# Two modulation maps of layer 1 summed by chains on VectorE instead of matmuls, with new ranks for the first feed-forward

## The chip, the cores and the metric

The kernel runs on one core of a Trainium2 chip. The metric is device time in microseconds (us) of one execution; the kernel before takes 2758.88 us in the median of 3 runs (2758.69 to 2758.89). Work is issued to five in-order engines: TensorE (PE, with its weight loads as PEld), VectorE (DVE), ScalarE (ACT), GpSimd (POOL) and SyncE (SP), which here issues all the transfers.

## The reference

The program is a trunk of two transformer layers over 1024 latent tokens and 256 context tokens, width 1024, in float32. Every layer first computes its modulation: six vectors of 1024 (shift, scale and gate for the attention and for the feed-forward) from one conditioning vector, once for the latent tokens and once for the context tokens.

```python
mod = silu_c @ w_mod[i] + b_mod[i]
mod_c = silu_cc @ w_mod[i] + b_mod[i]
sh1, sc1, gt1, sh2, sc2, gt2 = jnp.split(mod[:, None, :], 6, axis=-1)
sh1c, sc1c, gt1c, sh2c, sc2c, gt2c = jnp.split(mod_c, 6, axis=-1)
h = modulate(rmsnorm(x, g_attn[i]), sh1, sc1)
hc = modulate(rmsnorm(ctx, g_attn[i]), sh1c, sc1c)
```

So a map `v` (0 to 5) is a product of a row of 1024 with a matrix of 1024 x 1024. Layer 1 is the last layer. Its context tokens only deliver keys and values, so only the maps 0 and 1 (shift and scale of the attention) are needed for both rows, latent and context; the maps 2 to 5 are needed for the latent row alone.

After the attention, a layer has a gated feed-forward: an up-projection to 2 x 2816, a convolution over three positions, `a * silu(g)`, and a down-projection, for the latent tokens and in layer 0 for the context tokens too.

## The kernel before

Layer 0 and layer 1 each run in stages: attention, then the feed-forward. In the feed-forward of layer 0 (called ffn0) there follow each other the output projection of the attention, the context tokens' feed-forward (PE tiles `uc<-h2c` and `dnc`), the latent up-projection in 22 positions, and the down-projection in five sweeps.

Float32 weights are multiplied in three products: each weight block is loaded raw (`wraw`), rounded by ACT to its high part (`whi`) and its rest taken by DVE (`wlo`), and PE multiplies high by high, high by low and low by high. The up-projection also uses sums and differences of blocks (a fast scheme with seven block products in place of eight): per position DVE forms four sums `s`, takes the low parts of four weight blocks (`wlo`, three of 1024 columns and one of 512), and adds three products that come out of PSUM to the results `c`. PE runs 84 matmuls of 512 columns per position, named `ua`, `ud` and `uc`. Then `plan_u` (line 2017) makes the convolution: ACT starts a tile `u` from `c`, DVE adds the two other taps for both halves (four instructions on 1023 columns), ACT takes the SiLU, DVE multiplies, and DVE forms the blocks `ghit` and `glot` that go out to memory.

The tiles `c` and `u` come from one ring of eight slots (`x_tile`, line 1453, tag "x": the up results' ring). Raw loads come from a ring of three (`rpool`, line 280).

The maps of layer 1 are computed inside ffn0, under the up-projection. There are two ways to do it.

- By matmuls, `plan_mod` (line 405) with `mod_mm` (line 341): the activated conditioning vectors, padded to 32 columns (`cpad`), are the weights, and a 128-row slice of the matrix streams past them in four pieces of 256 columns. Two slices are loaded (`wm`), then eight matmuls of 32 x 256 run together; they sum up in a PSUM bank (`mod`). Eight slices make a map for both rows at once. The kernel before does maps 0 and 1 of layer 1 in this way (line 2084).
- By chains, `plan_mod_chain` (line 457): ACT multiplies the first slice by the conditioning value of each partition (`macc<-wm`), DVE adds the seven other slices times theirs with one SCALAR_TENSOR_TENSOR of 1024 columns each, and at the end four matmuls with a block of ones sum over the partitions (`mod<-macc,ones`). The kernel before does maps 2 to 4 in this way, for one row, with the running sum `macc` in one slot of the ring of eight.

In both ways ACT copies the bank, two transposes (`mod<-idr,modsb`) turn the sums, and DVE adds the bias (`modc`).

The order of all this is set when the program is built. A planner (`Sched`, line 97) takes every operation with an estimated duration and a key, lets each engine take the ready operation with the smallest key, and respects the slots of each ring; the engines then run in the order that comes out. `RANKS` (line 61) is a table of offsets to single operations' keys, one table for each stage, addressed by the number of the operation in the stage (applied at line 2261 for ffn0). All instructions go through one recording helper, so all of them carry its line, L51.

Of the kernel before, what the change touches and what calls it, by code (L numbers as in the profile page):

```python
# [11 lines left out]
F32 = mybir.dt.float32  # L12
# [5 lines left out]
P = 128  # L18
D = 1024
KT = 8  # L20
# [18 lines left out]
class InOrder:  # L39
# [7 lines left out]
    def __getattr__(self, name):  # L47
        f = getattr(self.eng, name)

        def call(*a, **k):  # L50
# [25 lines left out]
    ffn0={321: 16.4, 346: 3.3, 364: -15.4, 382: 3.9, 387: 4, 388: -8.1, 389: -5.4, 433: -24.5, 499: 13.3, 502: 17,  # L76
          503: -8.5, 519: 1.9, 548: 28.3, 571: 47.3, 1150: -18.3, 3223: -3.9, 3317: 2.1, 3398: 3.9, 3445: -3.9,
          3455: 9.6, 3469: 6.9, 3609: 20, 3613: 6.8},
    sw={6: -33, 8: -15, 11: 29.2, 14: 18.5, 67: -2.8, 73: -2.8, 74: 57.2, 141: -74.9, 152: 3.4, 162: 17.4, 168:
# [189 lines left out]
def trunk_kernel(ctx, tc, xperm, xtok, xseq, cc, wmod0, wmod, bmod, gnorm, na_wqkv, na_gq, na_gk, na_bias, na_wo,  # L269
# [3 lines left out]
    act, dve, pool, pe, dma = [InOrder(tc, e) for e in (nc.scalar, nc.vector, nc.gpsimd, nc.tensor, nc.sync)]  # L273

    cpool = ctx.enter_context(tc.tile_pool(name="const", bufs=1))
# [23 lines left out]
    dve.memset(cpad, 0.0)  # L299
    dma.dma_start(cpad[:, :, 0:2], cc)  # L300
    ones = cpool.tile([P, P], F32, name="ones")
    make_identity(nc, ones)
    idr = cpool.tile([P, P], F32R, name="idr")
    dve.tensor_copy(idr, ones)
# [842 lines left out]
    sc = Sched(dict(CAPS, klt=1))  # L1147
# [286 lines left out]
    def ffn(l, opj, xt1, todo):  # L1434
# [8 lines left out]
        sc = Sched(dict(b=8, raw=3, w=WBUFS, x=8, sr=SRB, g=GB, g2=GB, sq=2), {"b", "raw", "w", "x", "sr", "g", "g2", "sq"})  # L1443
# [6 lines left out]
        def bank(nm):  # L1450
            return ps.tile([P, 512], F32, tag="b", name=nm, bufs=8)

        def x_tile(nm):
            return fp.tile([P, 1024], F32, tag="x", name=nm, bufs=8)
# [18 lines left out]
        KU = KC + (8.8 * (FT + 1) if not last else 0.0)  # L1473
# [606 lines left out]
                plan_diffs()  # L2080
            plan_up(pos)
        if not last:
            for n in range(0, 16, 2):
                plan_mod(sc, 1, n // KT, n % KT, lambda: bank("mod"), "b", KU + 10 * n - 8, 3.0, True)
            for v in range(2, 5):
                plan_mod_chain(sc, v, 1, lambda: bank("mod"), "b", KU + 80 * v - 8, 10.0, 2.0, lambda: x_tile("macc"))
        else:
            plan_mod_chain(sc, 5, 1, lambda: bank("mod"), "b", KU + 150, 10.0, 2.0, lambda: x_tile("macc"))

# [297 lines left out]
    slabs = Slabs(sw_wqkv, WL1)  # L2387
    NSLAB = 2
    ffn(0, op0, None, [0, 1])
    gqk, sink, bandt, rc, rs = [C1[n] for n in ("gqk", "sink", "bandt", "rc", "rs")]  # L2390
    xs[1] = Parts([lo_part("x1", F32) for _ in range(4)], 2)
# [10 lines left out]
    sc = Sched(dict(CAPS, qraw=3, xl=4), {"raw"})  # L2402
# [403 lines left out]

    c1.close()
    ffn(1, op1, Parts(xt1, 4), [1])


# [93 lines left out]
def build(arrays):  # L2904
    import concourse.bacc as _bacc

    nc = _bacc.Bacc("TRN2", target_bir_lowering=False, num_devices=1, dynamic_dma_scratch_size=64)
    args = [nc.dram_tensor(f"in_{n}_dram", arrays[n].shape, mybir.dt.from_np(arrays[n].dtype), kind="ExternalInput").ap()
            for n in _INS]
    args.append(nc.dram_tensor("out_0_dram", (P, KT, T), F32, kind="ExternalOutput").ap())  # L2910
    with tile.TileContext(nc) as tc:
        trunk_kernel(tc, *args)
    return nc
# [10 lines left out]
```

## Time and profile before

| | before |
|---|---|
| median of 3 runs | 2758.88 us (2758.69 to 2758.89) |
| the profiled execution | 2759.63 us, its span 2757.8 us |
| granted TensorE clock | 0.999 |
| output projection of layer 0 | about 708 to 798 us of the span |
| context feed-forward of layer 0 | about 798 to 998 us |
| up-projection of layer 0 | about 985 to 1423 us |
| down-projection of layer 0 | about 1423 to 1634 us |

In the rows of the views, an instruction stands with its start, its duration, its engine, `out<-in`, the shape, and in brackets the idle time of its engine before it and what ended that. A duration is longer than the distance to the next instruction, because the next one starts before the last has drained; where a price is wanted, the distance between starts is the one to take. A busy share of PE counts those overlaps, so a busy PE need not be at its peak; the distance between starts tells that too.

### The profile page before, as it was taken

What the parts mean: (1) busy time and instruction counts of PE and PEld (TensorE: products, weight loads), DVE (VectorE), ACT (ScalarE), POOL (GpSimd) and SP (SyncE); (2) the same over time, 40 slices, a digit from 0 to 9 for tenths busy, and PEclk for the clock granted to TensorE, in tenths of its full rate; (3) what the DMA queues carried; (4) which work ended last, traced back from release to release, by engine and by line L of the source; (5) the groups of instructions that cost most, each with busy time, mean ns of one, the idle gap of its engine ahead of it and who ended that gap; (6) DMA issues with size and microseconds to landing.
All of it is one profiled execution on the core that took longest, in us unless ns stands there. A gap on an engine that the chain in (4) does not pass through costs nothing.

```text
span 2757.8 us, 45386 instructions
## 1 busy us (share of the span) xinstructions
PE 2731.3 (99%) x16073; PEld 2431.8 (88%) x16073; DVE 2291.1 (83%) x5005; ACT 1701.8 (62%) x3333; POOL 418.3 (15%) x684
## 2 busy tenths in 40 slices
PE   8999999999999999999999999999999999999999
PEld 7999999999889987788888888999988888888887
DVE  6888878888779678798998698888997989888766
ACT  6877777778556554455554457888874655555443
POOL 1222122223100000000000017546430000000000
PEclk9999999999999999999999999999999999999999
DMA  7222222224745544444476561010254234334745
GB/s 286 80 85 82 73 72 84 91 76 124 263 139 191 184 159 154 153 155 141 159 236 238 172 217 45 14 35 19 77 193 144 73 115 145 123 108 148 256 149 191
DMA packets 144868, 375.60 MB, mean 136 GB/s; under 512 B 22144, under 2 KB 35072, under 8 KB 143232
## 3 DMA queue, kind: packets, MB, share of 16 engines
q1 hardware_dynamic: 144640, 372.70, 40.8%
q8 instruction: 126, 2.06, 0.3%
q14 instruction: 102, 0.84, 0.1%
HBM read 305.59 MB, written 67.04 MB: 135 GB/s over the span
## 4 chain that ended last, share of the span: by engine, by line
PE 70%; DVE 3%; ACT 1%; issue 1%; DMA 0%; POOL 0%; SPq 0%; DVEq 0%; POOLq 0%; ACTq 0%
PE ua L51 17%; PE dn L51 15%; PE uc L51 12%; PE mm L51 6%; PE oacc L51 5%; PE ud L51 4%; PE pt L51 3%; PE pv L51 2%; PE s L51 2%; PE dnc L51 2%; PE u L51 1%; DVE S L51 1%; DVE ptlo L51 0%; PE mod L51 0%; DVE wlo L51 0%
## 5 line engine op out<-in xcount | busy, mean ns | idle before, releaser
L51 ACT ACTIVATE whi<-wraw 128x512 fp32r<-128x512 f32 (+1 forms) x264 | 212.9, 808 | 181.4 <-PE uc L51 55.2
L51 DVE TENSOR_TENSOR wlo<-wraw,whi 128x512 fp32r<-128x512 f32 (+1 forms) x264 | 240.5, 913 | 39.9 <-ACT whi L51 39.4
L51 DVE TENSOR_TENSOR ptlo<-pt,pthi 128x512 fp32r<-128x512 f32 (+2 forms) x384 | 223.0, 596 | 36.1 <-ACT pthi L51 33.8
L51 ACT ACTIVATE S<-S,m 128x640 f32<-128x640 f32 (+3 forms) x288 | 221.2, 770 | 35.8 <-DVE m L51 29.0
L51 PE MATMUL dn<-ghi,whi 128*128 128x512 f32 x616 | 239.9, 390 | 0.0
L51 PE MATMUL dn<-ghi,wlo 128*128 128x512 f32 x616 | 239.7, 389 | 0.0
L51 PE MATMUL dn<-glo,whi 128*128 128x512 f32 x616 | 239.6, 389 | 0.0
L51 ACT ACTIVATE pthi<-pt 128x512 fp32r<-128x512 f32 (+2 forms) x384 | 195.1, 524 | 55.1 <-PE pt L51 35.5
L51 DVE SCALAR_TENSOR_TENSOR u<-c,cv,u 128x1023 f32<-128x1023 f32 x176 | 222.2, 1279 | 3.4 <-ACT u L51 2.9
L51 ACT ACTIVATE whi<-s 128x1024 fp32r<-128x1024 f32 (+1 forms) x116 | 109.0, 940 | 164.0 <-PE uc L51 110.8
L51 ACT ACTIVATE ghi<-graw 128x512 fp32r<-128x512 f32 x154 | 96.4, 630 | 176.4 <-PE dn L51 103.5
L51 PE MATMUL pt<-idr,S 128*128 128x128 f32 x1280 | 195.2, 274 | 2.2 <-DVE qt L51 1.1
L51 PE MATMUL mm<-whi,h0hi 128*128 128x384 f32 x480 | 171.9, 358 | 0.4 <-ACT qraw L51 0.4
L51 DVE TENSOR_TENSOR glo<-graw,ghi 128x512 fp32r<-128x512 f32 x154 | 105.6, 689 | 72.0 <-ACT ghi L51 66.3
L51 PE MATMUL mm<-wlo,h0hi 128*128 128x384 f32 x480 | 162.0, 337 | 0.0
L51 PEld LDWEIGHTS pt<-idr,S 128*128 128x128 f32 x1280 | 149.6, 140 | 10.5 <-DVE ptlo L51 1.9
L51 POOL TENSOR_TENSOR qy<-qv,mhalf 128x4 f32<-128x4 f32 (+1 forms) x112 | 123.2, 1101 | 160.9 <-DVE qv L51 157.5
L51 POOL TENSOR_TENSOR n1y<-n1v,mhalf 128x4 f32<-128x4 f32 (+1 forms) x8 | 8.3, 1041 | 895.3 <-DVE n1v L51 895.3
L51 DVE TENSOR_TENSOR wlo<-s,whi 128x1024 fp32r<-128x1024 f32 (+1 forms) x116 | 124.4, 1075 | 21.3 <-ACT whi L51 21.1
L51 PEld LDWEIGHTS dn<-glo,whi 128*128 128x128 f32 x616 | 115.6, 188 | 24.1
L51 PEld LDWEIGHTS dn<-ghi,whi 128*128 128x128 f32 x616 | 115.6, 188 | 23.9
L51 PEld LDWEIGHTS dn<-ghi,wlo 128*128 128x128 f32 x616 | 115.6, 188 | 23.9
(392 smaller groups left out, 8856.0 us busy)
## 6 DMA issues: line engine op xcount, KB each, us to landing
wraw<-in_w_up_dram SPq DMA_DIRECT2D x132, 512.0 KB, 3.9
wm<-in_wmod_dram SPq DMA_DIRECT2D x80, 512.0 KB, 4.0
wraw<-in_w_down_dram SPq DMA_DIRECT2D x44, 512.0 KB, 3.8
graw<-g_dram SPq DMA_DIRECT2D x44, 512.0 KB, 4.5
wraw<-in_w_down_dram SPq DMA_DIRECT2D x88, 256.0 KB, 3.2
graw<-g_dram SPq DMA_DIRECT2D x66, 256.0 KB, 2.8
slab<-in_na_wqkv_dram SPq DMA_DIRECT2D x32, 384.0 KB, 3.8
woraw<-in_na_wo_dram SPq DMA_DIRECT2D x24, 512.0 KB, 4.5
```

Source lines behind the costliest of these rows:

```text
L51: r = f(*a, **k)
```

## The change

The two rows of maps 0 and 1 are now made by chains. Each of the two maps has two running sums, one for each row, and so two slots of the ring of eight; each of the slices 1 to 7 is added by two DVE instructions, and slice 0 is scaled by two ACT instructions. At the end eight matmuls sum over the partitions; so that the two rows land in the first and the second of the 32 columns, their weights are 32 columns out of a new tile `pick` of 33, which holds a column of ones among zeros. Maps 2 to 4 stay as they are. The table of ranks for ffn0 has 53 entries instead of 23, none of them kept with its value; the numbers that it refers to move too, because the chains have other operations than the matmuls had.

```diff
-    ffn0={321: 16.4, 346: 3.3, 364: -15.4, 382: 3.9, 387: 4, 388: -8.1, 389: -5.4, 433: -24.5, 499: 13.3, 502: 17,
...
+    ffn0={363: -13, 370: -3.9, 387: 24.1, 608: -73.6, 1117: 14.4, 1405: 25.9, 1438: -7.5, 1450: 26.8, 1480: -7.5,
...
     ones = cpool.tile([P, P], F32, name="ones")
+    pick = cpool.tile([P, 33], F32, name="pick")
+    dve.memset(pick, 0.0)
+    dve.memset(pick[:, 1:2], 1.0)
...
         if not last:
-            for n in range(0, 16, 2):
-                plan_mod(sc, 1, n // KT, n % KT, lambda: bank("mod"), "b", KU + 10 * n - 8, 3.0, True)
-            for v in range(2, 5):
-                plan_mod_chain(sc, v, 1, lambda: bank("mod"), "b", KU + 80 * v - 8, 10.0, 2.0, lambda: x_tile("macc"))
+            for v in range(5):
+                plan_mod_chain(sc, v, 2 if v < 2 else 1, lambda: bank("mod"), "b", KU + 80 * v - 8, 10.0, 2.0, lambda: x_tile("macc"))
```

The body of `plan_mod_chain` was there before, and is not changed. Its part for two rows, which ran in no program until now:

```python
for r in range(rows):
    def first(e, r=r, j=j):
        acc[r] = acc_tile()
        act.activation(acc[r], st[j], AF.Copy, scale=cpad[:, j, r:r + 1])

    def link(e, r=r, j=j):
        dve.scalar_tensor_tensor(out=acc[r], in0=st[j], scalar=cpad[:, j, r:r + 1], in1=acc[r], op0=ALU.mult, op1=ALU.add)
...
for r in range(rows):
    for g in range(4):
        pe.matmul(mod_acc[1, v][32 * g:32 * g + 32, :256], ones[:, :32] if rows == 1 else pick[:, 1 - r:33 - r],
                  acc[r][:, g * 256:(g + 1) * 256], start=r == 0, stop=r == rows - 1, skip_group_check=True)
```

What moves on the engines is shown at three places. On PE, in the early up-projection, a group of eight matmuls of the maps stands between products of two positions, once per position for eight positions; here is the first of the kernel before.

```order
L51 MATMUL ua_14387<-b22hi_14159,whi_14359 128x512
L51 MATMUL ua_14387<-b22lo_14173,whi_14359 128x512
L51 MATMUL ua_14387<-b22hi_14159,wlo_14360 128x512
L51 MATMUL mod_14372<-wm_14416,cpad_83 32x256 x4
L51 MATMUL mod_14372<-wm_14479,cpad_83 32x256 x4
L51 MATMUL ua_14540<-b1hi_11614,whi_14435 128x512
L51 MATMUL ua_14540<-b1lo_11625,whi_14435 128x512
```

All eight groups are gone, and after each of the two chains stands one group, here the first, with the two running sums as streams and the pick tile as weights.

```order
L51 MATMUL ua_14810<-t12lo_12256,whi_14838 128x512
L51 MATMUL ua_14810<-t12hi_12005,wlo_14839 128x512
L51 MATMUL mod_14963<-macc_14240,pick_87 32x256 x4
L51 MATMUL mod_14963<-macc_14252,pick_87 32x256 x4
L51 MATMUL ua_14810<-t12hi_12005,whi_14838 128x512
L51 MATMUL ua_14810<-t12lo_12578,whi_14838 128x512
```

The group stands in the fifth position, and the second one in the ninth; between positions 5 and 12 the products of neighbouring positions are also interleaved where they stood one position after the other before.

On DVE, a stretch around the convolution of the third position of the kernel before: low parts of weights (`wlo`), additions of products (`c`), taps of the convolution (`u`).

```order
L51 TENSOR_TENSOR wlo_14639<-s_14620,whi_14638 128x1024
L51 TENSOR_TENSOR c1_14609<-c1_14609,ua_14540 128x512
L51 TENSOR_TENSOR c1_14609<-c1_14609,uc_14604 128x512
L51 TENSOR_TENSOR wlo_14664<-s_14615,whi_14663 128x1024
L51 SCALAR_TENSOR_TENSOR u_14670<-c1_14609,cv_102,u_14670 128x1023
L51 TENSOR_TENSOR wlo_14685<-wraw_14556,whi_14684 128x512
L51 SCALAR_TENSOR_TENSOR u_14670<-c1_14609,cv_102,u_14670 128x1023
L51 SCALAR_TENSOR_TENSOR u_14692<-c0_14566,cv_102,u_14692 128x1023 x2
L51 TENSOR_TENSOR u_14692<-u_14692,u_14670 128x1024
L51 TENSOR_TENSOR c0_14719<-c0_14719,ud_14715 128x512
```

The same place of the changed kernel, with four links of the two chains (`macc`) in it.

```order
L51 SCALAR_TENSOR_TENSOR u_14689<-c0_14555,cv_105,u_14689 128x1023
L51 TENSOR_TENSOR wlo_14703<-wraw_14600,whi_14702 128x512
L51 TENSOR_TENSOR c0_14696<-c0_14696,ud_14692 128x512
L51 SCALAR_TENSOR_TENSOR u_14689<-c0_14555,cv_105,u_14689 128x1023
L51 SCALAR_TENSOR_TENSOR macc_14240<-wm_14667,cpad_83,macc_14240 128x1024
L51 TENSOR_TENSOR u_14689<-u_14689,u_14654 128x1024
L51 SCALAR_TENSOR_TENSOR macc_14252<-wm_14667,cpad_83,macc_14252 128x1024
L51 SCALAR_TENSOR_TENSOR macc_14240<-wm_14684,cpad_83,macc_14240 128x1024
L51 TENSOR_TENSOR glot_14761<-u_14689 128x512
L51 SCALAR_TENSOR_TENSOR macc_14252<-wm_14684,cpad_83,macc_14252 128x1024
L51 TENSOR_TENSOR c1_14735<-c1_14735,ua_14669 128x512
L51 TENSOR_TENSOR wlo_14748<-wraw_14721,whi_14747 128x1024
```

Twenty-eight links are added on DVE. The first stands just ahead of the first addition of a `ua` product to `c1`, the last nine positions later. If a position of DVE is counted from one addition `c1<-c1,uc` to the next, there are 31 links in the first ten positions; four of them are of map 2, as before.

On SP, which issues the transfers in order, the same place before: two raw weight blocks per position, and slices `wm` of the maps.

```order
L51 DMA wm_14479<-in_wmod_dram 128x1024
L51 DMA wraw_14544<-in_w_up_dram 128x1024
L51 DMA wraw_14556<-in_w_up_dram 128x1024
L51 DMA wm_14572<-in_wmod_dram 128x1024
L51 DMA g_dram_82<-u_14546 128x1024
L51 DMA g_dram_82<-ghit_14588 128x512
```

And in the changed kernel:

```order
L51 DMA wm_14667<-in_wmod_dram 128x1024
L51 DMA wm_14684<-in_wmod_dram 128x1024
L51 DMA wraw_14721<-in_w_up_dram 128x1024
L51 DMA g_dram_82<-u_14689 128x512
L51 DMA wraw_14766<-in_w_up_dram 128x1024
L51 DMA g_dram_82<-glot_14761 128x512
```

The number of loads is the same, 16 slices for the two maps. A slice's slot in the ring of three was free once eight matmuls had read it and its neighbour; now it is free once two DVE instructions have read it.

Outside of the up-projection the new ranks move instructions at two places: in the first third of the context feed-forward (where groups of `dnc` change places with groups of `uc`), and on DVE, ACT and SP in the second half of the down-projection and at its end. POOL's order is the same, and so is, but for the two memsets of `pick` at the kernel's start, every engine's order before the context feed-forward and from the start of layer 1's attention on.

More of the change, by code (lines that the diff above doesn't have):

```diff
@@ L75 @@
           9.4, 4766: 5.5, 4778: 5.9, 4788: 12.6, 4807: 5.2, 4811: -17.4, 4824: 10.3},
-    ffn0={321: 16.4, 346: 3.3, 364: -15.4, 382: 3.9, 387: 4, 388: -8.1, 389: -5.4, 433: -24.5, 499: 13.3, 502: 17,
-          503: -8.5, 519: 1.9, 548: 28.3, 571: 47.3, 1150: -18.3, 3223: -3.9, 3317: 2.1, 3398: 3.9, 3445: -3.9,
-          3455: 9.6, 3469: 6.9, 3609: 20, 3613: 6.8},
+    ffn0={363: -13, 370: -3.9, 387: 24.1, 608: -73.6, 1117: 14.4, 1405: 25.9, 1438: -7.5, 1450: 26.8, 1480: -7.5,
[6 rows of a table added]
     sw={6: -33, 8: -15, 11: 29.2, 14: 18.5, 67: -2.8, 73: -2.8, 74: 57.2, 141: -74.9, 152: 3.4, 162: 17.4, 168:
```

6 rows, old and new, of the table ffn0 are left out of this document.

## The prediction

> **What bounds the kernel now.** I read the page's busy times first, then the busy times by stretches of the up-projection, then single rows there.
>
> ```profile
> span 2757.8 us, 45386 instructions
> PE 2731.3 (99%) x16073; PEld 2431.8 (88%) x16073; DVE 2291.1 (83%) x5005; ACT 1701.8 (62%) x3333; POOL 418.3 (15%) x684
> ```
>
> PE is busy for 99% of the span, but overlaps hide small stalls, so I look at the rate. The next rows are busy times in two stretches of the up-projection of layer 0, each beginning and ending at the same place of a position: the first holds the eight matmul groups of the maps 0 and 1, the second one-row chains.
>
> ```profile
> core 0: us, PE busy (x) PEld busy (x) DVE busy (x) ACT busy (x) POOL busy (x), PEclk, DMA share, GB/s
> 1007.60:1170.50 162.90, 162.90 (x805) 129.19 (x804) 127.97 (x151) 78.58 (x96) 0.00 (x0) 1.00 0.44 152
> 1189.50:1399.50 210.00, 210.00 (x944) 172.12 (x943) 194.09 (x224) 109.27 (x134) 0.00 (x0) 1.00 0.48 159
> ```
>
> DVE is at 79% in the first and at 92% in the second; ACT is near half in both, and the clock is full. The timeline of DVE has one addition `c<-c,uc` per position; these are those of positions 1, 9 and 10.
>
> ```profile
> 1006.92 0.69 DVE L51 TENSOR_TENSOR c<-c,uc 128x512 f32<-128x512 f32 x1 [1.96 <-PE uc L51]
> ...
> 1169.83 0.69 DVE L51 TENSOR_TENSOR c<-c,uc 128x512 f32<-128x512 f32 x1 [2.03 <-PE uc L51]
> ...
> 1188.87 0.69 DVE L51 TENSOR_TENSOR c<-c,uc 128x512 f32<-128x512 f32 x1 [0.83 <-PE uc L51]
> ```
>
> A position without matmuls of the maps takes 1188.87 - 1169.83 = 19.04 us, 0.2267 us for each of its 84 matmuls. The eight with a group take 162.91 us, 20.36 each. So PE sets the pace, and DVE, though it is the fuller engine, waits for it. The Trainium skill would lead elsewhere: its page "Perfetto Trace Analysis", in "Identifying the Most-Contended Engine", asks to take an engine's occupancy for DVE and weight-load time, not matmul time, for PE; by that the bound in the second stretch is DVE (92% against 82%), and DVE should not be given more. Here the step of 0.2267 us decides against it as the traces stand, and the rival it makes comes below.
>
> **The matmuls removed.** This is the first group, among the products of PE.
>
> ```profile
> 1008.53 0.39 PE L51 MATMUL ua<-b22hi,wlo 128*128 128x512 f32 x1
> 1008.85 1.07 PE L51 MATMUL mod<-wm,cpad 128*32 128x256 f32 x16
> 1009.85 0.50 PE L51 MATMUL ua<-b22hi,whi 128*128 128x512 f32 x1
> 1010.19 0.40 PE L51 MATMUL ua<-b22lo,whi 128*128 128x512 f32 x1
> ```
>
> Its price is more than the 1.00 us between its start and the next `ua`, since the steps on both sides are long as well (0.32 and 0.34 against 0.23). I take it from the positions: 162.91 - 8 x 19.04 = 10.59, less two pairs of transposes at about 0.23, which stay, leaves 10.1, or 1.27 a group. Eight groups go and two come, one per chain, each with eight matmuls of the same shape (16 records): 6 x 1.27 = 7.6 us less on PE, all of it on the path, since PE runs without a gap there. The trace has no group with the pick tile; its ends are a one-row group of half as many matmuls and the removed one, and I take the latter, which has the same number of instructions; with half the price the saving would be 8.9.
>
> **The links added.** Rows of the tile `macc`, and of DVE around one link.
>
> ```profile
> L51 DVE SCALAR_TENSOR_TENSOR macc<-wm,cpad,macc x28: 1276/1280/1285, 1176.0 to 2356.8; 128x1024 f32<-128x1024 f32 x28
> L51 ACT ACTIVATE macc<-wm,cpad x4: 1135/1144/1146, 1162.2 to 2283.4; 128x1024 f32<-128x1024 f32 x4
> ```
>
> ```profile
> 1202.14 0.69 DVE L51 TENSOR_TENSOR s<-wraw 128x512 f32<-128x512 f32 x1
> 1202.74 1.28 DVE L51 SCALAR_TENSOR_TENSOR macc<-wm,cpad,macc 128x1024 f32<-128x1024 f32 x1
> 1203.94 0.69 DVE L51 TENSOR_TENSOR s<-s,wraw 128x512 f32<-128x512 f32 x1
> ...
> 1217.96 1.22 DVE L51 TENSOR_TENSOR wlo<-wraw,whi 128x1024 fp32r<-128x1024 f32 x1
> 1219.10 1.22 DVE L51 TENSOR_TENSOR u<-u 128x1024 f32<-128x1024 f32 x1
> ```
>
> From start to start a link costs DVE 1.20 us, an operation on 1024 columns 1.14, one on 512 0.60. The 28 links are 33.6 us of DVE work; the four new ACT instructions, 4.6 us, lie beside ACT's idle half. What a position asks of DVE without links: 3 x 1.14 + 0.60 for `wlo`, 4 x 0.60 for sums, 3 x 0.60 for product additions, 4 x 1.20 for taps, 1.14 for the product, and one or three blocks of 0.60: 15.4 on average. The changed order has 31 links in the first ten positions, so DVE must do 10 x 15.4 + 31 x 1.20 = 191 us there, where PE needs 10 x 19.04 + 2 x 1.27 + 0.5 = 193.4. DVE is at 99%. It fits, with 2.4 us over, if DVE hardly waits. These are its waits where it had one chain, over 220 us.
>
> ```profile
> DVE c L51 <- PE uc L51: 8.8, 10, 1.4
> DVE c L51 <- PE ua L51: 4.0, 6, 1.5
> DVE wlo L51 <- ACT whi L51: 2.1, 9, 0.6
> DVE modc L51 <- PE mod L51: 1.0, 1, 1.0
> ```
>
> 12.8 us of these are waits for PE's products, which a late DVE finds finished; the waits for ACT, 2.1 us, may stay. Then DVE has lateness, but lateness is not yet a stall: PE needs a `wlo` only when its product begins. So I added up both engines' rows in the changed order, at the steps above, from the last place that is the same in both kernels.
>
> ```profile
> 989.52 1.65 DVE L51 SCALAR_TENSOR_TENSOR uc<-uc,cv 128x255 f32<-128x255 f32 x4
> ...
> 1004.27 0.69 DVE L51 TENSOR_TENSOR c<-c,ua 128x512 f32<-128x512 f32 x1 [0.25 <-PE ua L51]
> ```
>
> ```profile
> 984.58 0.40 PE L51 MATMUL ua<-b1hi,whi 128*128 128x512 f32 x1
> ```
>
> Without any wait of DVE, each `wlo` is ready before PE needs it; the least reserve is near 3 us, first in the seventh position (about 1092 us) and again up to about 1167, and the two pick groups find their chains ready with 4 and 3 us to spare. From these come off the waits that DVE cannot avoid because PE has not got there: it would reach the addition at 1004 some 3.5 us too early, and one near 1085 by 1.3. So PE is late by some 1.8 us at the seventh position; with waits for ACT between none and their 2.1 the stall is 1.8 to 4. I take 2.9. It is paid once: after a stall PE's needs are later too, and after the tenth position the order is the old one, at 92%.
>
> **What is taken at nothing.** The slices are as many as before, and SP stays in order; but a slot of the three is now freed by DVE.
>
> ```profile
> SPq L51 <- DVE macc L51: 43.7, 20, 4.3
> SPq L51 <- PE mod L51: 39.0, 8, 8.5
> wraw<-in_w_up_dram SPq DMA_DIRECT2D x132, 512.0 KB, 3.9
> wm<-in_wmod_dram SPq DMA_DIRECT2D x80, 512.0 KB, 4.0
> ```
>
> SP's waits for links were not longer than for matmuls (first two rows). In the changed order the shortest way from the last reading of a slot to the first use of the next load is 4.7 us of DVE rows in the steady part, against 4.0 for the landing and 0.3 for the issue. It is covered, by 0.4; if a load comes 1 us late, `s` waits on DVE and the stall grows by that. Two slots of the ring of eight go to the sums, where one did not hold PE up; with six left I take 0, and an upper end of a position's late copies belongs to the slow rival. The two memsets at the start lie in 7 us of DVE's idle time. The reordered groups of the context part and of the down-projection: PE there is as full as can be.
>
> ```profile
> 8.21 0.17 DVE L51 TENSOR_SCALAR nv<-nv 128x2 f32<-128x2 f32 x1 [7.05 <-ACT junk L51]
> 820.00:825.00 5.00, 4.87 (x41) 4.66 (x40) 5.00 (x11) 4.42 (x7) 0.00 (x0) 1.00 0.45 127
> 1580.00:1620.00 40.00, 40.00 (x186) 33.36 (x185) 38.31 (x67) 21.97 (x37) 1.39 (x1) 1.00 0.58 180
> 1635.63 0.47 PE L51 MATMUL mm<-whi,h1chi 128*128 128x512 f32 x1 [0.24 <-ACT whi L51]
> ```
>
> What new ranks can win there is the 0.13 us of idle time at 820 and the 0.24 at 1635; what they can lose is a conversion or two put late in a stretch where DVE is at 96%, 1.2 us. I take 0 between -0.4 and +1.2.
>
> **Sum.** -7.6 + 2.9 = -4.7 us. The profiled execution had a span of 2757.8, so its span becomes 2753.1; the median of the runs shown is 2758.88, 1.1 more than that span, so the forecast is 2754.2.
>
> **Rivals.** *No stall at all.* If ACT and the loads are always early and the reserve is larger than my sums make it, only the matmuls show: 2758.9 - 7.6 = 2751.3, and 2750 with a cheaper pick group and 0.4 from the ranks. For it speaks the second stretch, where DVE was at 92% and PE's step did not grow; against it, that DVE is not seen fuller than 38.31 of 40 us in any row above.
>
> *DVE becomes the bound.* DVE works in order, and a link put ahead of a `wlo` holds it; if its idle share stays as it was in the second stretch, (210 - 194.09) / 210 = 7.6%, because each wait handed on to ACT comes back to it, the first eleven positions ask 11 x 15.4 + 33 x 1.20 = 209 us of DVE, and take 209 / 0.924 = 226.2 instead of PE's 212.5: 13.7 us of stall, +6.1 net, 2765. It decides for slower from an idle share of about 7.4%. For it speaks that the waits were spread over many rows, against it that most of them were for PE itself. This is the case that the Trainium skill's rule on the most-contended engine would have; on the trace so far it bears out the fullness of DVE, and not that PE's step follows it.
>
> *The ranks decide.* The stall is as forecast, and the moved groups outside of the up-projection cost their 1.2 us or win 0.4: 2753.8 to 2755.4. It is no other sign, only a spread.
>
> **How the numbers follow.** Two runs of this kernel can be told apart from about 0.2%, or 5.5 us; that is 2753.4 on the one side and 2764.4 on the other. The forecast case, with the ranks' spread, gets 0.45, of which a tenth reaches below 2753.4. No stall, or less than 2.1 us of it, gets 0.31 more. DVE as the bound gets 0.24: 0.16 of it beyond 2764.4, 0.08 in milder form between 2757 and 2764. So faster 0.35, same 0.49, slower 0.16. The range reaches from the cheap end of no stall, 2750, to 2764, where the last rival begins to be slower.
>
> **What would show it.** PE should have 2 groups with `pick` of about 1.07 us and no `mod<-wm` of layer 1's; the eight positions from 1006.92 on should take about 152.3 + 3 + the stall, or 158 us, instead of 162.9. DVE should be above 97% between about 1005 and 1190, with its waits for `uc` gone. PE's waits for `wlo` should appear, at the seventh position or later, 2 to 4 us together. Weight loads show the same: they took 172.12 of 210 us, 82%, where PE had its full step, and stretches below that are stalls. I am wrong if DVE still idles 5% there while PE waits (then it is order, not load), if `s` waits for `wraw` more than 2 us in total, or if the stages after 1430 differ by more than 1.2 us.

## The result: slower by 0.3%, lost in the down-projections

The changed kernel takes 2768.03 us in the median of seven runs (2765.39 to 2769.39), the kernel before 2758.88 (2758.03 to 2761.88) beside it: a ratio of the means of 1.0030, with a 95% interval of 1.0019 to 1.0042. The profiled execution took 2768.26 us, 8.6 more than that of before. The first two rows of its page:

```profile
span 2766.5 us, 45202 instructions
...
PE 2738.3 (99%) x15977; PEld 2432.7 (88%) x15977; DVE 2321.2 (84%) x5035; ACT 1704.1 (62%) x3337; POOL 419.0 (15%) x684
```

DVE has 30 us more, and PE is busy for 7 us more although 96 of its matmul records are gone. So I go by the times between fixed places of the trace, in both executions (and in three of the experiments below):

| us | before | after | e1_pad_only | e2_pick512 | e6_right352 |
|---|---|---|---|---|---|
| up-projection of layer 0, first `c<-c,uc` to last | 414.0 | 410.8 | 414.0 | 410.9 | 410.4 |
| down-projection of layer 0, first `dn` to first `mm<-whi,h1chi` | 212.2 | 217.7 | 217.7 | 212.2 | 212.1 |
| from there to the first `dn` of layer 1 | 909.0 | 910.0 | 908.9 | 908.7 | 908.4 |
| down-projection of layer 1, first `dn` to last | 209.2 | 214.8 | 214.7 | 209.2 | 209.2 |

The up-projection, where the chains are, is 3.2 us shorter. These are its rows on DVE in the changed kernel (the additions that end positions 1, 9 and 10), and the busy times in the two stretches that answer to those of the prediction.

```profile
1006.60 0.68 DVE L51 TENSOR_TENSOR c<-c,uc 128x512 f32<-128x512 f32 x1
...
1164.54 0.69 DVE L51 TENSOR_TENSOR c<-c,uc 128x512 f32<-128x512 f32 x1
...
1185.38 0.69 DVE L51 TENSOR_TENSOR c<-c,uc 128x512 f32<-128x512 f32 x1
```

```profile
core 0: us, PE busy (x) PEld busy (x) DVE busy (x) ACT busy (x) POOL busy (x), PEclk, DMA share, GB/s
1006.60:1164.54 157.94, 155.53 (x688) 126.98 (x688) 152.72 (x171) 75.63 (x94) 0.00 (x0) 0.99 0.43 146
1185.38:1395.00 209.62, 209.62 (x942) 171.81 (x941) 196.00 (x224) 109.17 (x134) 0.00 (x0) 1.00 0.50 163
```

Eight positions take 157.94 us in place of 162.91, with DVE at 96.7%; and PE, which had no idle time there, now has 2.4 us. Only one of the two groups with `pick` lies in them; the second comes behind them, in the ninth position, which takes 20.84 us in place of 19.04:

```profile
1167.83 1.07 PE L51 MATMUL mod<-macc,pick 128*32 128x256 f32 x16
```

The two down-projections are 5.5 and 5.6 us longer. Layer 1's has the same instructions in the same order as before. What is different is the pace of the matmuls: here are all the `dn` matmuls of both layers, with the shortest, the median and the longest duration in ns, first before and then after.

```profile
L51 PE MATMUL dn<-ghi,whi x616: 389/389/486, 1423.4 to 2753.3; 128*128 128x512 f32 x154
L51 PE MATMUL dn<-glo,whi x616: 387/389/396, 1423.7 to 2753.6; 128*128 128x512 f32 x154
L51 PE MATMUL dn<-ghi,wlo x616: 388/389/398, 1423.9 to 2753.8; 128*128 128x512 f32 x154
```

```profile
L51 PE MATMUL dn<-ghi,whi x616: 387/392/484, 1419.9 to 2762.0; 128*128 128x512 f32 x154
L51 PE MATMUL dn<-glo,whi x616: 388/394/405, 1420.2 to 2762.2; 128*128 128x512 f32 x154
L51 PE MATMUL dn<-ghi,wlo x616: 387/399/399, 1420.4 to 2762.4; 128*128 128x512 f32 x154
```

The medians rise from 389 to 392, 394 and 399. From start to start the mean step goes from 226.7 ns to 232.7, and 1,848 matmuls x 6.0 ns = 11.1 us, which is the whole of 5.5 + 5.6. PE has no gap there and the granted clock is 1.00 in both. The matmuls of the up-projections (`ua`, `ud`, `uc`, as wide as these) keep 226.7.

What distinguishes `dn`? In the built programs the new tile `pick` takes 160 bytes a partition among the constants at the lower end of SBUF, and everything on that (left) side lies 160 bytes higher than before: the weights `whi` start at 89,280 and not at 89,120. The right side has not moved: `ghi` is at 155,168 in both. The operands of `ua`, `ud` and `uc` all lie on the left, and have moved together; in 1,320 of the 1,848 `dn` matmuls the weights have moved and `ghi` or `glo` has not. The other 528 read `ghi` and `glo` tiles on the left. They come in spells of twelve among the others, and their step comes back to 226.7 ns from the ninth matmul of a spell on, while the 1,320 have a mean of about 234. That made the first theory: the pace follows the distance in SBUF between the two operands. The rival was that the new order, or the fuller DVE, slows the down-projections in some way.

### The profile page after: what moved, and what is told of

It reads as the page before. It is cut to its first block, busy times and chain, and to the rows that moved or that the text cites. A ratio compares the mean times of both kernels' runs of the same rounds, so it can differ in the third digit from the quotient of the medians.

```text
span 2766.5 us, 45202 instructions
## 1 busy us (share of the span) xinstructions
PE 2738.3 (99%) x15977; PEld 2432.7 (88%) x15977; DVE 2321.2 (84%) x5035; ACT 1704.1 (62%) x3337; POOL 419.0 (15%) x684
## 4 chain that ended last, share of the span: by engine, by line
PE 94%; DVE 3%; ACT 1%; DMA 1%; issue 1%; POOL 0%; SPq 0%; DVEq 0%; ACTq 0%; POOLq 0%
PE mm L51 18%; PE ua L51 16%; PE dn L51 15%; PE uc L51 13%; PE pt L51 7%; PE pv L51 6%; PE s L51 5%; PE oacc L51 5%; PE ud L51 4%; PE dnc L51 2%; PE u L51 1%; DVE S L51 1%; PE mod L51 0%; DMA wm<-in_wmod_dram 0%; DVE ptlo L51 0%
## 5 line engine op out<-in xcount | busy, mean ns | idle before, releaser
L51 ACT ACTIVATE S<-S,m 128x640 f32<-128x640 f32 (+3 forms) x288 | 221.3, 770 | 35.9 <-DVE m L51 28.1
L51 PE MATMUL ua<-t12hi,whi 128*128 128x512 f32 x336 | 132.0, 393 | 2.4 <-ACT c L51 2.4
```

The lines of the kernel that those rows point to most:

```text
L51: r = f(*a, **k)
```

## The experiments

### The tile alone, and the same tile with another size

e1_pad_only is the kernel before, with a tile that nobody reads:

```diff
     ones = cpool.tile([P, P], F32, name="ones")
+    pad = cpool.tile([P, 33], F32, name="pad")
+    dve.memset(pad, 0.0)
```

> The kernel before with one more tile of 128x33 beside the identity, zeroed at the start and read by nothing; no chain, no rank is touched. It moves what lies on the left side of SBUF up by 160 bytes a partition, as the change's pick tile does: the weights whi and wlo among it, but not the ghi and glo of the right side that they are multiplied with. Theory (addresses): the matmuls of the down-projections follow at 0.2335 us in place of 0.2267 (some 6 ns more for each of 1,848), and the time is 2770, between 2768 and 2772. Rival (the new order of the ranks or the longer DVE list slows the down-projections): nothing changes, 2758.9 and steps of 0.2267.

It takes 2771.0 us (2768.1 to 2771.7), 1.0043 of the kernel before (1.0029 to 1.0056). One of its rows:

```profile
L51 PE MATMUL dn<-ghi,wlo x616: 387/399/399, 1422.5 to 2763.3; 128*128 128x512 f32 x154
```

The same median as in the changed kernel, the same 217.7 and 214.7 us in the table above, and the up-projection is unchanged at 414.0. An unused tile of 132 bytes costs 12 us. e2_pick512 is the changed kernel with a `pick` of 512 bytes:

```diff
-    pick = cpool.tile([P, 33], F32, name="pick")
+    pick = cpool.tile([P, 128], F32, name="pick")
```

> The changed kernel with the pick as 128x128 and not 128x33, so that the left side moves by 512 bytes and not by 160. Order, ranks and instructions stay those of the changed kernel. Theory (addresses, with 512 bytes as a distance that does no harm): steps of 0.2267 us in both down-projections, 5.5 us back in each, and 2757, between 2755 and 2758, so faster than the kernel before. Rival (order): 2768, as the changed kernel.

It takes 2756.44 us (2753.50 to 2757.47), 0.9990 of the kernel before (0.9981 to 0.9999).

```profile
L51 PE MATMUL dn<-ghi,wlo x616: 388/389/397, 1421.9 to 2751.6; 128*128 128x512 f32 x154
```

Both down-projections are back at their times of before, to 0.1 us, with the new order and the new ranks. The rival falls on both sides. e4_pad64 asked for the unit, with a tile of 64 bytes in the kernel before:

```diff
+    pad = cpool.tile([P, 16], F32, name="pad")
+    dve.memset(pad, 0.0)
```

> The kernel before with a tile of 128x16 (64 bytes a partition) in the place of the pick, read by nothing. Theory (addresses): if what counts is the place within 64 bytes, the steps stay at 0.2267 us and the time at 2759; if it is the place within 128, 256 or 512 bytes, the steps go to 0.230 to 0.2335 and the time to 2765 to 2770. Rival (order): 2759 and 0.2267.

The `dn` step was 231.9 ns and the time 2764.4 us in its one execution: a multiple of 64 bytes is not enough. It had a surprise with it: the context part's matmuls `dnc`, with 256 columns, went from 120.0 to 114.5 ns.

### Distance, or the place of each operand?

e6_right352 leaves the `pick` of the changed kernel as it is, and moves the other operand after it:

```diff
+    gap = spool.tile([P, 88], F32, name="gap")
+    dve.memset(gap, 0.0)
```

> The changed kernel with its pick of 128x33 left as it is, and an unused tile of 352 bytes a partition at the head of SBUF's right side, so that weights and ghi, glo are a multiple of 512 bytes apart again, while all of the left side stays moved by 160. Theory (distance): steps of 0.2267 us in both down-projections, and 2756.4 as with the pick of 128x128, between 2754 and 2758. Rival (the place of the weights by itself): 2768, or some 2764.

2756.09 us (2754.03 to 2757.92), 0.9988 of before (0.9978 to 0.9997), with the `dn` medians at 389 again:

```profile
L51 PE MATMUL dn<-ghi,wlo x616: 388/389/397, 1420.9 to 2750.2; 128*128 128x512 f32 x154
```

So it is not where the weights lie, but how far from the moving operand. e5_offsets measured that by itself, in one execution: bursts of 48 matmuls and nothing beside them.

```diff
+    def burst(name, n, xo, wo, reps):
+        o = ps.tile([P, 512], F32, tag="o", name=name)
+        for i in range(reps):
+            for a, (xk, wk) in enumerate(((0, 0), (1, 0), (0, 1))):
+                xs, ws = xo // 4 + 1024 * xk, wo // 4 + 2048 * wk + 128 * (i % 8)
+                pe.matmul(o[:, :n], w[:, ws:ws + P], x[:, xs:xs + n], ...)
```

> A kernel of matmuls alone, in place of the whole computation (its output is a constant): bursts of 48 matmuls like those of the down-projection, three to a weight pair, with 512, 384, 256 and 128 columns, in which only the place of the moving operand against the weights changes, by steps of 32 bytes, and some in which the weights or both are moved. Theory (distance): the step between matmuls follows the distance of the two operands modulo 512 bytes; with 512 columns it is 0.2267 us at distance 0, about 0.2335 at 352 (the changed kernel) and 0.233 at 448, and for both moved together again 0.2267. Rival (place of each operand by itself): moving both is as slow as moving one. Third possibility, no effect without the other engines: 0.2267 everywhere.

The mean step in ns of the last 36 matmuls of each burst, by how far the moving operand was put up in bytes:

| columns | 0 | 32 | 64 | 96 | 128 | 160 | 192 | 224 |
|---|---|---|---|---|---|---|---|---|
| 512 | 226.7 | 233.3 | 228.8 | 233.4 | 233.4 | 234.3 | 233.4 | 233.4 |
| 384 | 173.3 | 173.3 | 173.3 | 176.7 | 176.0 | 173.3 | 174.7 | 173.3 |
| 256 | 120.0 | 117.8 | 117.8 | 120.1 | 118.7 | 118.7 | 117.8 | 118.3 |
| 128 | 111.7 | 111.8 | 111.7 | 111.7 | 111.6 | 111.7 | 111.7 | 111.7 |

From 256 to 480 bytes the row repeats itself within 0.1 ns; with 512 columns, 512 and 1024 bytes give 226.7 again, and 4, 8, 16 and 24 bytes give 236.6, 233.3, 231.7 and 233.3. Moving the weights alone by 32, 64 or 160 bytes gives 233.3 to 233.4; moving both by as much gives 226.7 each time. The rows of the last two groups (four distances each, `w512o` with the weights moved, of which one is 256 bytes, and `b512o` with both):

```profile
L289 PE MATMUL w512o<-x,w x192: 387/394/447, 541.8 to 618.9; 128*128 128x512 f32 x192
...
L289 PE MATMUL b512o<-x,w x192: 389/389/398, 553.0 to 629.7; 128*128 128x512 f32 x192
```

So the distance counts, modulo 256 bytes and not 512 as I had expected, and it needs no other engine. In the changed kernel it had gone from 0 to -160, which is 96: 233.4 here, about 234 there.

### What held PE up in the up-projection

The saving there should have been 7.6 us, and 3.2 are seen. These are PE's and then ACT's rows at the one large gap of the changed kernel.

```profile
1094.21 0.39 PE L51 MATMUL uc<-t34h,wlo 128*128 128x512 f32 x1
1096.68 0.50 PE L51 MATMUL ua<-t12hi,whi 128*128 128x512 f32 x1 [2.09 <-ACT c L51]
...
1098.73 0.63 PE L51 MATMUL ua<-t12lo,whi 128*128 128x512 f32 x1
1099.16 0.63 PE L51 MATMUL ua<-t12hi,wlo 128*128 128x512 f32 x1
```

```profile
1090.65 2.18 ACT L51 ACTIVATE macc<-wm,cpad 128x1024 f32<-128x1024 f32 x2
1092.74 0.57 ACT L51 ACTIVATE c<-ua 128x512 f32<-128x512 f32 x1
1093.96 1.06 ACT L51 ACTIVATE u<-u 128x1024 f32<-128x1024 f32 x1 [0.65 <-DVE u L51]
1094.92 1.23 ACT L51 ACTIVATE u<-c,cv 128x1024 f32<-128x1024 f32 x1
1096.06 0.57 ACT L51 ACTIVATE c<-ua 128x512 f32<-128x512 f32 x1
```

PE goes on adding to the bank `ua` of the next position only after ACT has copied the sum of its first product out (`c<-ua`), and that copy stands behind other work of ACT. Behind the gap eight matmuls take about 0.43 us a step and not 0.23: the granted clock is lower there.

```profile
1097.00:1100.00 3.00, 3.00 (x10) 2.34 (x9) 3.00 (x4) 0.58 (x1) 0.00 (x0) 0.67 0.55 178
```

The gap is 2.25 us beyond the normal step and the slow matmuls are 8 x 0.2 = 1.6, together 3.9 of the 4.4 us that are missing; another 0.5 is a gap at 1139. For the cause there were four candidates: DVE's load, the slots of the ring, ACT's first multiplications, and the order itself. The next three kernels ran once each, and all are made on e2_pick512. e7_no_links took away DVE's load, with the order kept; the slices 1 to 7 are left out of the sums:

```diff
                 def link(e, r=r, j=j):
+                    if rows == 2:
+                        return
                     dve.scalar_tensor_tensor(out=acc[r], in0=st[j], ...)
```

> The pick of 128x128, with the order of the changed kernel, but the 28 links of maps 0 and 1 are not computed (the slices 1 to 7 of the two maps of layer 1 are left out of the sums). Theory (the stall is DVE's lateness handed on through ACT): from the first c<-c,uc of the up-projection to the last 414.0 - 7.6 = 406.4 us, in place of 410.9 with links and 414.0 before, no wait of PE for ACT's c, and 2752. Rival (the stall comes from the new order or from the ring of eight, in which the sums still take their slots): 410.9 and 2756.

```profile
1095.90 0.63 PE L51 MATMUL ua<-t12hi,whi 128*128 128x512 f32 x1 [2.10 <-ACT c L51]
```

410.5 us from the first `c<-c,uc` to the last, and 2755.24: without 33.6 us of DVE work the large gap is the same, and only the small one at 1139 is gone. My theory fell. e9_no_slots took away the slots of the sums and ACT's first multiplications as well (the groups with `pick` read another tile, and the order is planned anew); e10_pool_zero took ACT's first multiplications away, and kept links and slots.

```diff
                 def first(e, r=r, j=j):
+                    if rows == 2:
+                        return
...
-                          acq=[("x", I + ("acc", r), 1)], rel=[I + ("raw", j)])
+                          acq=[("x", I + ("acc", r), 1)] if rows == 1 else (), rel=[I + ("raw", j)])
```

> As the run without links, and the sums of maps 0 and 1 take no slots of the ring of eight either (neither the first multiplications nor the links are computed, the eight matmuls with the pick read another tile; layer 1's first two maps are not computed). The planner puts the order together anew, with the same ranks. Theory (the stall comes from the ring: with two to four slots gone, the copies c<-ua are placed behind the SiLU that frees a slot): no wait of PE for ACT's c in the seventh position, 406.4 us from the first c<-c,uc to the last, in place of 410.5 with the slots taken. Rival (the stall is the new order's as such, whatever the ring): 410 or more.

```diff
                 def first(e, r=r, j=j):
+                    if rows == 2:
+                        pool.memset(acc[r], 0.0)
+                        return
```

> The changed kernel with the pick of 128x128, its order and its links, but the first multiplication of a sum is not ACT's: GpSimd sets the sum to zero in its place (slice 0 of maps 0 and 1 is left out). So ACT is free of the 2.18 us that stand ahead of the copy c<-ua that PE waits for. Theory (the ring; ACT's copy waits behind the SiLU for DVE): the gap of 2.1 us stays, 410 us from the first c<-c,uc to the last. Rival (ACT's first multiplications hold the copy back): no gap, 407.

The row of the gap in e9_no_slots, and that in e10_pool_zero:

```profile
1096.25 0.51 PE L51 MATMUL ua<-t12hi,whi 128*128 128x512 f32 x1 [2.10 <-ACT c L51]
...
1096.84 0.40 PE L51 MATMUL ua<-t12hi,wlo 128*128 128x512 f32 x1
1097.07 0.40 PE L51 MATMUL ua<-t12hi,whi 128*128 128x512 f32 x1
```

```profile
1096.68 0.50 PE L51 MATMUL ua<-t12hi,whi 128*128 128x512 f32 x1 [2.10 <-ACT c L51]
```

In e9_no_slots the gap stayed, and of what e7_no_links had left only the slow matmuls behind it went: 409.0 us and 2754.1. The theory of the ring fell with that. In e10_pool_zero nothing changed: 410.9 and 2756.0. So it is neither the ring nor ACT's first multiplications. What is left is the order itself. In the kernel before, the last product of a position (`ua<-b22`) was followed by 24 matmuls of the next (`ua<-b1`, `ud<-b1`) that wait for none of these copies; the new order has run those earlier, and has nine matmuls there, 2.04 us, against a round trip of ACT: copy 0.57, wait for DVE's taps, SiLU 1.06, the second `u<-c,cv` 1.23, copy 0.57. e12_silu_after_copy puts the SiLU of this one position behind the copy (it is made on e11_context_64, below):

```diff
                 sc.op("act", t_act(1024), center, ...)
+                late = not last and ft == 2
+                if late and not part:
+                    sc.op("act", t_act(1024), lambda e: act.activation(V[1], V[1], AF.Silu), reads=[v], ...)
...
-                if part:
+                if part and not late:
                     sc.op("act", t_act(1024), lambda e: act.activation(V[1], V[1], AF.Silu), ...)
```

> The version with the pick of 128x64 and the shifted operands of the context part, and in one position (the third channel block, at about 1095 us) ACT's SiLU u<-u is put behind the second u<-c,cv and the next position's copy c<-ua; beside it some rows within the next position change places. Theory (the gap is a round trip of ACT, with 0.57 for the copy, the wait for DVE's taps and 1.06 for the SiLU, 1.23 for u and 0.57 for the next copy, behind nine matmuls of PE that take 2.04): without the SiLU and its wait ahead of the copy the gap of 2.1 us falls to about 0.4, and the slow matmuls behind it shrink with it: 410.5 becomes 407 to 409 from the first c<-c,uc to the last, and 2748 to 2750. Rival (another wait takes its place at once, since DVE's product u waits for the SiLU): 410 to 412, and 2751 to 2753.

```profile
1090.54 0.50 PE L51 MATMUL ua<-t12hi,whi 128*128 128x512 f32 x1 [0.55 <-ACT c L51]
...
1094.65 0.50 PE L51 MATMUL ua<-b1hi,wlo 128*128 128x512 f32 x1 [0.60 <-DVE wlo L51]
```

The gap falls to 0.55 us and the slow matmuls are gone; the next waits, 0.60 for a `wlo` and 0.69 for a copy some 40 us later, give part of it back. From first to last `c<-c,uc` it is 408.4 us in place of 410.5. The round trip was the cause. The whole does not show it: 2751.01 us (2750.14 to 2751.91), 0.9969 of before (0.9957 to 0.9981), where its base had 2751.41 and I had forecast 2748 to 2750. In the profiled execution the stretch with layer 1's attention, in which nothing was meant to change, took some 2.5 us more than in the base, with gaps of 0.54 us (0.20 in the base) and 0.96 (none there); what they come from I did not settle.

### What the table of ranks is worth

e3_pick512_oldranks keeps the chains and a `pick` of 512 bytes, with the old table; e8_no_ranks has an empty one, and ran once.

```diff
-    ffn0={363: -13, 370: -3.9, 387: 24.1, ...
+    ffn0={321: 16.4, 346: 3.3, 364: -15.4, ...
```

> As the run with the pick of 128x128, and the feed-forward's table of ranks is the one of the kernel before, so that the chains alone are left of the change. Theory (addresses; the ranks only place the stall of the up-projection): steps of 0.2267 us in the down-projections, and the up-projection 7.6 us shorter less a stall of another size, 2 to 8 us: 2751 to 2760. Rival (the new ranks carry the loss): 2755 here and 2768 in the run with the new ranks.

```diff
-    ffn0={363: -13, 370: -3.9, 387: 24.1, ...
+    ffn0={},
```

> The pick of 128x128 with the table of ranks for the first feed-forward empty. Theory: the table keeps conversions ahead of PE's need; without it the up-projection has more stalls, 5 to 25 us more than the 410.9 of the changed order, and 2760 to 2780. Rival (the ranks hardly matter, and the old table, 2787, was harmful because its numbers fall on other operations): within 3 us of 2756.4.

2787.1 us (1.0103 of before, 1.0089 to 1.0117) and 2778.6. I had given the old table 2751 to 2760: its numbers now fall on other operations, and it is worse than none. In the up-projection the two lose nearly the same, 17.9 and 18.5 us against the changed order; what sets them apart is layer 0's down-projection, which takes 221.3 us with the old table and 211.8 with none. The loss of the up-projection comes in a few long waits of PE, at about 1079, 1144 and 1229 us. In e8_no_ranks they are, from 1000 to 1430 us (engine, line, what for: us in total, times, longest):

```profile
PE ua L51 <- DVE wlo L51: 8.5, 3, 6.0
...
PE ua L51 <- ACT whi L51: 7.4, 2, 3.7
```

With the new ranks there is no wait of PE for `wlo` at all.

### A version that beats both

For 256 columns a distance of 0 is among the slowest. e11_context_64 gives the changed kernel a `pick` of 256 bytes, and moves only the operands of the context part: `h2c` by 64 bytes, its `ghi` and `glo` by 192.

```diff
-    pick = cpool.tile([P, 33], F32, name="pick")
+    pick = cpool.tile([P, 64], F32, name="pick")
...
+    def hc_tile(s, dt, nm, k, at=None):
+        n, o = dict(hi=(2064, 0), lo=(2096, 48))[s]
+        o = o if at is None else at
+        return hpool.tile([P, n], dt, tag=f"hc{s}", name=nm, bufs=1)[:, o:o + 2048].rearrange("p (k n) -> p k n", k=k)
...
-                    act.activation(G[ft][0][:, :256], st[0], AF.Copy)
+                    act.activation(G[ft][0][:, 48:304], st[0], AF.Copy)
```

> A version for use: the changed kernel with the pick as 128x64 (256 bytes), and the moving operands of the context feed-forward, which have 256 columns, placed at a distance from the weights that is no multiple of 256 bytes: h2c at 64, ghi and glo of dnc at 192 modulo 256; all that has 512 columns stays at 0. Theory (distance, from the offsets run and from the run with 64 bytes): dn steps of 0.2267, dnc 0.1145 in place of 0.1200 (528 matmuls, 2.9 us), uc of the context 0.1178 or less (1,056 matmuls, 2.3 us or more), so 5 to 8 us less than 2756.4: 2750, between 2747 and 2753. Rival (the context part is bound by ACT and DVE, which were full there): 2756.

2751.41 us (2750.70 to 2755.07), 0.9975 of the kernel before (0.9965 to 0.9985). The `dnc` row of e2_pick512, and that of this version:

```profile
L51 PE MATMUL dnc<-ghi,whi x176: 277/283/283, 815.2 to 999.4; 128*128 128x256 f32 x176
```

```profile
L51 PE MATMUL dnc<-ghi,whi x176: 275/277/282, 814.0 to 994.2; 128*128 128x256 f32 x176
```

The steps are 115.0 ns for `dnc` and 117.9 for the context's `uc`, both 120 before: 528 x 5.0 + 1,056 x 2.2 = 5.0 us, and 2756.44 - 2751.41 is 5.0.

## Why the prediction was wrong

**The failed step is among "what is taken at nothing".** The prediction counted the new tile `pick` by its two memsets, which lie in idle time, and did not ask where the tile puts everything that is allocated after it. It moved the weights against the operands of the down-projections: +5.5 and +5.6 us, shown from both sides by e1_pad_only (the tile without the change, +12) and by e2_pick512 and e6_right352 (the change without the shift). "I am wrong if the stages after 1430 differ by more than 1.2 us" was the sentence that caught it. Without the shift the change takes 2756.4 and 2756.1 us, against the forecast of 2754.2; of the 2 us between, 1.5 are the stall, which is larger than forecast, and the rest is less than the spread of e2_pick512's runs (2753.5 to 2757.5).

**The bound.** PE's pace did set the time in the up-projection. DVE went to 96.7% (the prediction said more than 97%), and 33.6 us of its work taken away again in e7_no_links changed 0.3 us. The rule that the prediction quoted from the Trainium skill, page "Perfetto Trace Analysis", section "Identifying the Most-Contended Engine", would have had DVE as the bound, by weight-load time (the section names a second measure for TensorE, MFU, the matmul work done as a share of the peak, which the prediction did not take); the runs of this order don't bear that out.

**The matmuls removed, 7.6 us.** Borne out: e9_no_slots, with nothing of the chains but their eight-matmul groups, wins 5.0 of 414.0 us with a gap that costs 2.25, together 7.3.

**The stall, 2.9 us between 1.8 and 4.** Its place was right (about 1092 us forecast, 1094 seen), its size low: 4.4 us are missing in all. That looked like a near hit until e7_no_links. The mechanism was wrong: PE has no wait for a `wlo`, which the prediction named as the sign; what it waits for is ACT's copy, in a round trip that the new order leaves uncovered. I had added up engines against each other's needs for `wlo`, and had not asked what PE waits for within one bank. That the eight positions took 157.94 us, against the 158 forecast, is luck: that sum put both groups with `pick` into them, and only one is there, so that the stall in them is 157.94 - 152.3 - 1.5 = about 4.1 us and not 2.9, and it has another cause.

**The ring, ACT's four instructions, the ranks, at nothing.** The ring and ACT: right as far as the large gap goes, which stays without them in e9_no_slots and e10_pool_zero; why the slow matmuls went in e9_no_slots is open. The ranks' moved rows in the down-projection: 212.2 us before and in e2_pick512, so 0. The wait of `s` for `wraw` came to 2.8 us, over the 2 that I had named, but it is one wait at 997 us, ahead of the first link; within the eight positions there is none, where the kernel before had three, 2.5 us together. So the loads kept up with the chains.

**The rivals.** "DVE becomes the bound" gave 2765, near the measured time, and was not what happened: that it comes close is luck. Under another order PE does wait for `wlo` and `whi`, in e8_no_ranks; but DVE is idle for 9% there (busy for 387.05 of 424 us), so by the prediction's own sign that is order and not load. "No stall at all" was wrong too, as the gap shows. And the new table was no spread of 1 us but a condition of the change.

## What to carry to other kernels

A tile added to a pool moves all that is allocated after it on its side of SBUF: before a small change is judged, put the addresses of both operands of the busiest matmuls side by side, and make the new tile a size that keeps their distance (here a multiple of 256 bytes). When a loss shows in a stage with the same instructions in the same order, look at the step from start to start; busy shares and gaps showed nothing here. A stall where it was forecast may still have another cause; taking the suspected load away, with the order kept, costs one run.

## What was not expected of the hardware

The step of float32r matmuls depends on the distance in SBUF between the moving operand and the weights, modulo 256 bytes: 226.7 ns at 0 and 231.7 to 236.6 elsewhere (228.8 at 64) for 512 columns, the other way round for 256 columns (120.0 at 0 and 120.1 at 96, 117.8 at 32, 64 and 192), and without any effect for 128 (111.6 to 111.8). No other engine computed beside these bursts, and they ran in one execution. The Trainium skill, page "SBUF — State Buffer", section "Who interferes with whom", gives PE two independent read ports, one for the moving operand and one for weight loads; in e5_offsets the step depends on how the places of the two operands lie to each other, so in effect the two reads are not independent; by what mechanism stays open. In the kernel `dnc` gained more at 192 (114.5 to 115.0) than in the bursts (117.8); why is open.

A gap of PE of 2.1 us was followed by eight matmuls at about 0.43 us in the changed kernel (granted clock 0.67 from 1097 to 1100 us), in e7_no_links and in e10_pool_zero, and by none in e9_no_slots, after a gap as long. They begin at once in e7_no_links and some 1.3 us behind the gap in the changed kernel. So the length of the gap alone does not decide.
